# A transformer trunk on one core: the first product behind each LayerNorm, taken part by part in an order set by hand

## The chip, the cores and the metric

One NeuronCore of a Trainium2 chip runs the whole program in one launch. The metric is the device time of one execution in microseconds. The engines are TensorE (PE for matmuls and PEld for its weight loads), VectorE (DVE), ScalarE (ACT), GpSimd (POOL) and SyncE (SP), which issues nearly all DMAs; each engine works through a list of its own, whose order is fixed when the program is compiled.

## What is computed

256 tokens of width 1024 pass through two layers. Layer 0 is a latent attention (MLA), layer 1 a sparse attention whose keys an indexer selects (DSA). Each is followed by PEER, a mixer that finds experts by product keys. Behind each of the four comes a LayerNorm of the residual sum:

```python
for i in range(DEPTH):
    m = _mla_mixer(x, ...) if i % N_MIXERS == 0 else _dsa_mixer(x, ...)
    x = _layernorm(DN_ALPHA * x + m, ln_gain[i, 0], ln_bias[i, 0])
    f = _peer(x, peer_w_q[i], peer_sub_keys[i], peer_w_down[i], peer_w_up[i])
    x = _layernorm(DN_ALPHA * x + f, ln_gain[i, 1], ln_bias[i, 1])
```

`_layernorm` is `(x - mean) * rsqrt(var + eps) * g + b` over the 1024 columns. The first thing that the next mixer does with x is a product: `_peer` has `xt @ w_q`, `_dsa_mixer` has `x @ w_in`.

## The kernel before

**Products in three parts.** Every float32 operand of a large product is held as a rounded high half and a low half, the remainder. A product is then high x high + high x low + low x high, three matmuls into the same PSUM accumulator. `mm` (line 195) issues a matmul.

**The weight stream.** All weights pass through `Stream` as blocks of 128 x 1024 (512 KB), in one fixed order. A block is loaded by SyncE into one of four raw buffers (line 73), ScalarE copies it to the high half (line 85), and raw minus high gives the low half (line 88). There are four buffers each for raw, high and low. A raw buffer is free again when its low split is done; a high or low buffer when TensorE has read it for the last time. The low split runs on VectorE, except that GpSimd takes it for `TO_POOL` = 2 blocks from the moment when the first norm of a pair is written, and for every third block in part of DSA. `ws.get` takes the next block and fills ahead.

**The output products.** `rows` (line 231) multiplies both token tiles (128 tokens each, t = 0 and 1) with one weight block, six matmuls of 512 columns per tile, into four PSUM accumulators y. The last `STAGGER` = 4 blocks are handled in `finish` (line 259): all four for tile 0 first, then all four for tile 1, so that the norm of tile 0 can run beside the products of tile 1.

**The norm.** `layernorm` works on one tile: two halves of the residual sum with their row sums (VectorE, line 248), the negative mean (250), the sum of squares (ScalarE, 251) and the centred rows times the gain (VectorE, 252), the variance (253), its power of -1/2 (GpSimd, 254), and two halves of the result (VectorE, 257).

**The joint.** After a norm, `xpose` turns the tile for the next product: eight TensorE transposes in two groups of four (line 225), each group copied to the high half xh (ScalarE, 211), and its low half xl taken by VectorE (212). The tile is also stored to DRAM (line 229). Then comes the first product of the next stage on its first four weight blocks, `FIRST` = 4: the values of DSA (v, first lines of `dsa`) or the first 512 query columns of PEER (qw, in `peer`). There tile 0 takes its 24 matmuls with all three parts block by block, then tile 1 its 24. There are three such joints: MLA to PEER 0 (joint 1, at about 101 us), PEER 0 to DSA (joint 2, 931 us), DSA to PEER 1 (joint 3, 1071 us). The fourth norm ends in the stores of the output.

In PEER, a query tile is copied to SBUF (line 595), turned by four transposes (qwT, 598), copied again (599), and multiplied with the keys (ps); the keys are loaded at line 584 into memory that the norm's bias held until then. The products on blocks 4 and on follow (pq in PEER; more of v in DSA).

**What sets the order.** The program is written stage by stage; the compiler's list scheduler then orders the instructions of each engine by a simulated time and the dependencies, so an instruction can stand ahead of one that was written earlier. `tc.issue_after(ins)` adds an edge: what is issued in its block stands behind `ins` on the same engine. Before, it is used only to put the last products of tile 1 behind those of tile 0, and around some loads.

Of the kernel before, what the change touches and what calls it, by code (L numbers as in the profile page):

```python
# [22 lines left out]
CHUNK = 64  # L23
DEPTH = 2
HEADS = 8
NKEYS = 128
# [3 lines left out]
ALPHA = (2 * DEPTH) ** 0.25  # L30
LN_EPS = 1e-5
# [9 lines left out]
CELLS = sum(SEG)  # L41
STAGGER = 4
STEPS = (2, 1)
TO_POOL = 2
FIRST = 4
GSCALE = 2.0 ** 14
TINY = 2.0 ** -40
# [4 lines left out]
class Stream:  # L52
# [5 lines left out]
    def __init__(self, nc, raw, hi, lo):  # L58
        self.nc, self.raw, self.hi, self.lo = nc, raw, hi, lo
        self.blocks, self.ready = [], []  # L60
        self.n_loaded = self.n_split = self.n_taken = 0
        self.tiles = []
        self.to_pool = 0
        self.share = 0

    def add(self, src, w=D):
# [10 lines left out]
    def _split(self, upto):  # L77
        nc = self.nc
        while self.n_split <= min(upto, len(self.blocks) - 1):
            w = self.blocks[self.n_split][1]  # L80
            self._load(self.n_split)
            raw = self.tiles[self.n_split][:, :w]
            hi = self.hi.tile([P, D], F32R, tag="hi", name=f"hi{self.n_split}")[:, :w]
            lo = self.lo.tile([P, D], F32R, tag="lo", name=f"lo{self.n_split}")[:, :w]
            nc.scalar.copy(hi, raw)  # L85
            eng = nc.gpsimd if self.to_pool > 0 or (self.share and self.n_split % self.share == 0) else nc.vector
            self.to_pool -= 1
            eng.tensor_tensor(lo, raw, hi.bitcast(F32), op=ALU.subtract)  # L88
            self.ready.append((hi, lo))
            self.n_split += 1  # L90

    def get(self, ahead=None):
        i = self.n_taken
        self.n_taken += 1
        self.fill(i + (self.AHEAD if ahead is None else ahead))
        return self.ready[i]

    def fill(self, upto):
        self._split(upto)
# [31 lines left out]
def tile_trunk(ctx: ExitStack, tc: tile.TileContext, ins, out: bass.AP):  # L131
    nc = tc.nc
# [6 lines left out]
    small = pool("small", 3)  # L139
# [22 lines left out]
    xl = const.tile([P, NC, T], F32R, tag="xl", name="xl")  # L162
# [14 lines left out]
    ws = Stream(nc, raws, his, los)  # L177
# [32 lines left out]
    def split_ps(hi, lo, p):  # L210
        nc.scalar.copy(hi, p)
        return nc.vector.tensor_tensor(lo, p, hi.bitcast(F32), op=ALU.subtract)
# [4 lines left out]
            nc.sync.dma_start(xs[t], src[t])  # L217
        return xs

    def xpose(t, x):  # L220
        for g in range(2):
            p = ps(f"xt{t}{g}")
            for j in range(4):
                c = 4 * g + j
                nc.tensor.transpose(p[:, j * P : (j + 1) * P], x[:, c * P : (c + 1) * P], ident)
            pv = p.rearrange("p (j t) -> p j t", t=P)
            cs, tsl = slice(4 * g, 4 * g + 4), slice(t * P, (t + 1) * P)
            split_ps(xh[:, cs, tsl], xl[:, cs, tsl], pv)
        nc.sync.dma_start(keep[t], x)

    def rows(o4, lhs, blk, start, stop, tiles=(0, 1)):

        h, l = blk
        lh, ll = lhs
        for t in tiles:
            tsl = slice(t * P, (t + 1) * P)
            todo = [(w, rr, i, n) for i, (w, rr) in enumerate(((lh, h), (lh, l), (ll, h))) for n in range(2)]
            if stop:
                todo.sort(key=lambda z: z[3])
            for w, rr, i, n in todo:  # L240
                ins = mm(o4[t][n], w[:, tsl], rr[:, n * 512 : (n + 1) * 512], start and i == 0, stop and i == 2)
        return ins

    def layernorm(x, y2, g, b, r, z, sq):
        st = small.tile([P, 6], F32, tag="st", name="st")
        for n in range(2):
            s = slice(n * 512, (n + 1) * 512)
            nc.vector.scalar_tensor_tensor(r[:, s], x[:, s], ALPHA, y2[n], op0=ALU.mult, op1=ALU.add,
                                           accum_out=st[:, n : n + 1])
        nc.vector.tensor_scalar(st[:, 2:3], st[:, 0:1], st[:, 1:2], -1.0 / D, op0=ALU.add, op1=ALU.mult)  # L250
        nc.scalar.activation(sq, r, AF.Square, bias=st[:, 2:3], accum_out=st[:, 3:4])
        nc.vector.scalar_tensor_tensor(z, r, st[:, 2:3], g, op0=ALU.add, op1=ALU.mult)
        nc.vector.tensor_scalar(st[:, 4:5], st[:, 3:4], 1.0 / D, LN_EPS, op0=ALU.mult, op1=ALU.add)  # L253
        nc.gpsimd.tensor_tensor(st[:, 5:6], st[:, 4:5], mhalf, op=ALU.pow)  # L254
        for n in range(2):
            s = slice(n * 512, (n + 1) * 512)
            nc.vector.scalar_tensor_tensor(r[:, s], z[:, s], st[:, 5:6], b[:, s], op0=ALU.mult, op1=ALU.add)

    def finish(y4, lhs_of, n, g, b, x, spare, after):

        blks = [ws.get(ahead=0) for _ in range(STAGGER)]
        last = None
        for t in range(2):
            with ExitStack() as order:
                if last is not None:
                    order.enter_context(tc.issue_after(last.ins))
                for i, blk in enumerate(blks):
                    k = n - STAGGER + i
                    last = rows(y4, lhs_of(k), blk, k == 0, k == n - 1, (t,))
            layernorm(x[t], y4[t], g, b, spare[t], spare[2 + t], spare[4])  # L270
            if t == 0:
                ws.to_pool = TO_POOL
            after(t, spare[t])

    def load_affine(ar, li, which):
        g, b = ar.take(D), ar.take(D)
# [63 lines left out]
    def out_proj(oh, ol, g, b, x, spare):  # L340
        y4 = [[py(2 * t + n, f"y{t}{n}") for n in range(2)] for t in range(2)]
        for h in range(HEADS - STAGGER):
            rows(y4, (oh[:, h, :], ol[:, h, :]), ws.get(), h == 0, False)
        finish(y4, lambda h: (oh[:, h, :], ol[:, h, :]), HEADS, g, b, x, spare, xpose)

    def load_mask(ar):
        m = ar.take(384)
# [132 lines left out]
    def dsa():  # L480
# [24 lines left out]
        for t in range(2):  # L505
# [8 lines left out]
        p = ps("ki")  # L514
# [50 lines left out]
    def peer(li):  # L565
# [17 lines left out]
        tail = s[0].rearrange("p a b -> p (a b)")  # L583
        nc.sync.dma_start(keys, ins["keys"][li].rearrange("n p k -> p n k"))

        first = [ws.get(ahead=0) for _ in range(FIRST)]
        for t in range(2):
            tsl = slice(t * P, (t + 1) * P)
            p = py(t, f"qw{t}")
            for i, (h, l) in enumerate(first):  # L590
                for j in range(2):
                    c = 2 * i + j
                    half_ = slice(j * 512, (j + 1) * 512)
                    mm3(p, (xh[:, c, tsl], xl[:, c, tsl]), (h[:, half_], l[:, half_]), c == 0, c == NC - 1)
# [4 lines left out]
            nc.scalar.copy(qT[:, 0:4, tsl], p.rearrange("p (n t) -> p n t", t=P))  # L599

        for g4 in range(4):
            for j in range(0, 4 if g4 else 0, 2):
# [158 lines left out]
                g, b = load_affine(lnar, li, 1)  # L761
        spare = [lnar.take(D) for _ in range(5)]

        def store(t, x):
            for n, q in enumerate((nc.sync, nc.scalar)):
                s = slice(n * 512, (n + 1) * 512)
                q.dma_start(out[t * P : (t + 1) * P, s], x[:, s])

        finish(y4, operand, NKEYS, g, b, x, spare, store if last else xpose)

    ws._load(0)
    xt = Arena(arena, 30720).take(NC, T)
# [83 lines left out]
```

## Time and profile before

| | |
|---|---|
| median of 3 runs | 1911.16 us (1910.89 to 1911.22) |
| the profiled execution | 1910.36 us |
| its span | 1908.6 us, 33303 instructions |
| mean granted clock of TensorE | 0.996 |
| TensorE busy with matmuls | 1860.4 us (97%) |
| VectorE | 1358.9 us (71%) |
| ScalarE | 1059.9 us (56%) |
| GpSimd | 582.0 us (30%) |
| DMA | 335.51 MB, mean 176 GB/s |

The span is the stretch from the first to the last instruction of the profiled execution; its time also holds what lies around that, 1.8 us. Matmuls overlap one another, so the busy time of a matmul (some 0.39 us for 512 columns) is longer than the step from one to the next, and the steps have to be read from the starts. A granted clock of 1.00 is 2.4 GHz, 0.50 is 1.2 GHz.

### The profile page before, as it was taken

How to read it: one execution, taken by the hardware profiler on the slowest of the kernel's cores; microseconds unless marked ns; L12 is line 12 of the kernel's file. 1: busy time of each engine (PE TensorE's matmuls, PEld its weight loads, DVE VectorE, ACT ScalarE, POOL GpSimd, SP SyncE). 2: the span in 40 equal slices, each digit the busy share in tenths (PEclk: the TensorE clock that was granted, in tenths of full speed). 3: DMA queues.
4: the chain of work that ended last, by engine and by line, in shares of the span. 5: the costliest groups of instructions: out<-in, count | busy, mean ns of one | idle time of the engine just before them, and what ended most of it. 6: DMA issues, size and time to landing. Idle time of an engine off the chain costs nothing.

```text
span 1908.6 us, 33303 instructions
## 1 busy us (share of the span) xinstructions
PE 1860.4 (97%) x12482; PEld 1674.4 (88%) x12482; DVE 1358.9 (71%) x2765; ACT 1059.9 (56%) x1837; POOL 582.0 (30%) x654
## 2 busy tenths in 40 slices
PE   8989999999999999999998899999999999999998
PEld 8779999999998888888798799999999988888886
DVE  5579998788766555555669689997788765555555
ACT  6544446777655444444466444558777554444443
POOL 2011336999620000000123103359997400000000
PEclk9999999999999999999999999999999999999999
DMA  6354455444446555555554544554444465555553
GB/s 230 120 201 166 154 169 186 156 155 156 166 172 232 190 190 188 188 187 188 183 180 155 172 149 165 179 184 147 155 156 166 167 229 189 188 189 189 190 189 114
DMA packets 93762, 335.51 MB, mean 176 GB/s; under 512 B 10400, under 2 KB 11424, under 8 KB 93600
## 3 DMA queue, kind: packets, MB, share of 16 engines
q1 hardware_dynamic: 93312, 332.87, 50.7%
q8 instruction: 97, 1.59, 0.3%
q14 instruction: 65, 0.53, 0.1%
q10 hardware_dynamic: 288, 0.52, 0.1%
HBM read 329.16 MB, written 4.19 MB: 175 GB/s over the span
## 4 chain that ended last, share of the span: by engine, by line
PE 63%; issue 25%; DVE 7%; POOL 3%; ACT 1%; DMA 1%; SPq 0%; DVEq 0%; POOLq 0%; ACTq 0%
PE d L195 30%; PE y L195 19%; PE pq L195 4%; POOL VU L694 3%; PE G L195 3%; DVE lo L88 2%; PE qw L195 1%; PE v L195 1%; DVE arena L653 1%; PE q L195 1%; PE h L195 1%; PE ps L195 1%; DVE arena L648 1%; PE qi L195 1%; PE qn L195 0%
## 5 line engine op out<-in xcount | busy, mean ns | idle before, releaser
L88 DVE TENSOR_TENSOR lo<-raw,hi 128x1024 fp32r<-128x1024 f32 x593 | 755.4, 1276 | 336.4 <-ACT hi L85 335.4
L85 ACT CAST hi<-raw 128x1024 fp32r<-128x1024 f32 x604 | 631.5, 1048 | 589.4 <-PE y L195 225.2
L195 PE MATMUL d<-xh,lo 128*128 128x256 f32 x2048 | 581.4, 284 | 8.2 <-DVE lo L88 8.2
L195 PE MATMUL d<-xh,hi 128*128 128x256 f32 x2048 | 586.3, 286 | 0.0
L195 PE MATMUL d<-xl,hi 128*128 128x256 f32 x2048 | 579.5, 283 | 0.0
L694 POOL TENSOR_SCALAR VU<-iota,i2t 128x128 f16<-128x128 f16 x512 | 425.8, 849 | 82.0 <-PE G L195 57.4
L195 PEld LDWEIGHTS d<-xh,lo 128*128 128x128 f32 x2048 | 386.7, 189 | 11.0 <-DVE lo L88 11.0
L195 PEld LDWEIGHTS d<-xh,hi 128*128 128x128 f32 x2048 | 387.1, 189 | 0.0
L195 PEld LDWEIGHTS d<-xl,hi 128*128 128x128 f32 x2048 | 386.9, 189 | 0.0
L195 PE MATMUL y<-lo,xh 128*128 128x512 f32 x1088 | 345.2, 395 | 0.0
L195 PE MATMUL y<-hi,xh 128*128 128x512 f32 x1088 | 344.7, 395 | 0.0
L195 PE MATMUL y<-hi,xl 128*128 128x512 f32 x1088 | 344.5, 395 | 0.0
L254 POOL TENSOR_TENSOR st<-st,mhalf 128x1 f32<-128x1 f32 x8 | 4.5, 557 | 863.1 <-DVE st L253 863.1
L195 PEld LDWEIGHTS y<-lo,xh 128*128 128x128 f32 x1088 | 204.8, 188 | 48.0 <-DVE lo L88 0.6
L195 PEld LDWEIGHTS y<-hi,xl 128*128 128x128 f32 x1088 | 205.0, 188 | 47.9
L195 PEld LDWEIGHTS y<-hi,xh 128*128 128x128 f32 x1088 | 204.9, 188 | 47.5
L695 DVE TENSOR_SCALAR VU<-iota,i1t,gt 128x128 f16<-128x128 f16 x512 | 139.3, 346 | 73.2 <-PE G L195 55.4
L696 ACT ACTIVATE U<-VU,gr 128x128 f16<-128x128 f16 x512 | 170.9, 397 | 0.9 <-DVE VU L695 0.5
L750 ACT CAST xh<-arena 128x512 fp32r<-128x512 f32 x128 | 79.3, 620 | 153.1 <-PE y L195 147.8
L751 DVE TENSOR_TENSOR xl<-arena,xh 128x512 fp32r<-128x512 f32 x128 | 88.3, 692 | 80.7 <-ACT xh L750 80.7
L650 POOL TENSOR_TENSOR arena<-arena 128x800 f32<-128x800 f32 x32 | 72.6, 2274 | 96.7 <-DVE arena L648 89.2
L195 PE MATMUL G<-VU 128*128 128x128 f16 x512 | 73.8, 222 | 4.4 <-DVE VU L695 2.2
(220 smaller groups left out, 1869.9 us busy)
## 6 DMA issues: line engine op xcount, KB each, us to landing
raw<-in_down SPq DMA_DIRECT2D x256, 512.0 KB, 3.2
raw<-in_up SPq DMA_DIRECT2D x256, 512.0 KB, 4.2
raw<-in_peer_q SPq DMA_DIRECT2D x32, 512.0 KB, 4.1
raw<-in_dsa_qk SPq DMA_DIRECT2D x16, 512.0 KB, 3.2
raw<-in_mla_w_o SPq DMA_DIRECT2D x8, 512.0 KB, 4.0
raw<-in_dsa_v SPq DMA_DIRECT2D x8, 512.0 KB, 4.1
raw<-in_dsa_w_o SPq DMA_DIRECT2D x8, 512.0 KB, 4.4
raw<-in_mla_qk SPq DMA_DIRECT2D x7, 512.0 KB, 4.8
```

The costliest lines, as they stand in the source:

```text
L85: nc.scalar.copy(hi, raw)
L88: eng.tensor_tensor(lo, raw, hi.bitcast(F32), op=ALU.subtract)
L195: return nc.tensor.matmul(o, l, r, start=start, stop=stop, skip_group_check=True)
L254: nc.gpsimd.tensor_tensor(st[:, 5:6], st[:, 4:5], mhalf, op=ALU.pow)
L648: nc.vector.tensor_tensor(o, iota[:, None, :CELLS].to_broadcast([P, TOPK, CELLS]), posf[t][:, h, :, None].to_broadcast([P, TOPK, CELLS]), ...
L650: nc.gpsimd.tensor_tensor(o, o, cell[t][:, h, None, :].to_broadcast([P, TOPK, CELLS]), op=ALU.mult)
L653: nc.vector.tensor_reduce(exp_[t][:, h - 1, :], held, axis=AX.X, op=ALU.add)
L694: nc.gpsimd.tensor_scalar(V, iota16, i2t[:, t : t + 1], None, op0=ALU.is_equal)
L695: nc.vector.tensor_scalar(U, iota16, i1t[:, t : t + 1], gt[:, t : t + 1], op0=ALU.is_equal, op1=ALU.mult)
L696: nc.scalar.mul(L, U, gr[:, t : t + 1])
L750: nc.scalar.copy(hh, a)
L751: nc.vector.tensor_tensor(al, a, hh.bitcast(F32), op=ALU.subtract)
```

## The change

`TO_POOL` and the counter `to_pool` go: at the joints GpSimd takes no low split any more. `layernorm` becomes the class `Norm`, `xpose` the class `Turned`, with the same instructions, cut into steps that are called one by one. Each step issues through `queue`, which puts every instruction behind the one before it on the same engine (for TensorE, VectorE and ScalarE). `Stream.open` takes a block and issues only its high split, `Stream.close` issues the low split and the load that the raw buffer was kept from. `finish` gets `lead`, which is `lead_queries` or `lead_values` and gives the matmuls of one tile, part and block ("hh", "lh", "hl": first letter the half of x, second the half of the weights), and writes the whole joint out. `dsa` and `peer` take over accumulators that are already begun; in `peer` both query tiles are copied and turned after all 48 matmuls. At the kernel's end (`lead is None`) the two norms follow one another and the stores come behind both.

```diff
-            eng = nc.gpsimd if self.to_pool > 0 or (self.share and self.n_split % self.share == 0) else nc.vector
-            self.to_pool -= 1
+            eng = nc.gpsimd if self.share and self.n_split % self.share == 0 else nc.vector
...
+    def open(self, queue):
+        i = self.n_split
+        self._load(i)
+        raw = self.tiles[i]
+        hi = self.hi.tile([P, D], F32R, tag="hi", name=f"hi{i}")
+        lo = self.lo.tile([P, D], F32R, tag="lo", name=f"lo{i}")
+        queue("act", lambda: self.nc.scalar.copy(hi, raw))
...
+    def close(self, i, queue):
+        hi, lo = self.ready[i]
+        queue("dve", lambda: self.nc.vector.tensor_tensor(lo, self.tiles[i], hi.bitcast(F32), op=ALU.subtract))
+        self._load(i + self.DMA_AHEAD + 1)
...
+    def queue_of():
+        last = {}
+        def queue(engine, emit):
+            with ExitStack() as order:
+                if engine in last:
+                    order.enter_context(tc.issue_after(last[engine]))
+                ins = emit()
+            last[engine] = ins.ins
+            return ins
+        return queue
...
-            layernorm(x[t], y4[t], g, b, spare[t], spare[2 + t], spare[4])
-            if t == 0:
-                ws.to_pool = TO_POOL
-            after(t, spare[t])
+            norms.append(Norm(queue, x[t], y4[t], g, b, spare[t], spare[2 + t], spare[4]))
+        n0, n1 = norms
+        n0.sums()
+        n0.centre()
+        n0.scale()
+        n0.result()
+        if lead is None:
...
+            return
+        nc.sync.dma_start(keep[0], spare[0])
+        queue("pe", lambda: last)
+        x0, x1 = Turned(queue, 0, spare[0]), Turned(queue, 1, spare[1])
+        blk = [ws.open(queue) for _ in range(3)]
+        n1.sums()
+        x0.high(0)
+        x0.high(1)
+        n1.centre()
+        blk.append(ws.open(queue))
+        x0.low(0)
+        n1.scale()
+        x0.low(1)
+        n1.result()
+        nc.sync.dma_start(keep[1], spare[1])
+        unit = lead(queue)
...
+        do(0, "hh", 0, 1, 2)
+        do(0, "lh", 0, 1, 2)
+        do(0, "hh", 3)
+        do(0, "lh", 3)
+        x1.high(0)
+        x1.high(1)
+        do(1, "hh", 0, 1, 2, 3)
+        ws.close(blk[0], queue)
+        ws.close(blk[1], queue)
+        x1.low(0)
+        do(0, "hl", 0, 1)
+        do(1, "lh", 0, 1)
+        do(1, "hl", 0, 1)
+        ws.close(blk[2], queue)
+        x1.low(1)
+        do(0, "hl", 2)
+        do(1, "hl", 2)
+        do(1, "lh", 2)
+        ws.close(blk[3], queue)
+        do(0, "hl", 3)
+        do(1, "hl", 3)
+        do(1, "lh", 3)
...
+    def lead_values(queue):
+        v4 = [[py(2 * t + n, f"v{t}{n}") for n in range(2)] for t in range(2)]
...
+        def unit(t, part, k, blk):
+            l, w = operands(t, part, k, blk)
+            for n in range(2):
+                queue("pe", lambda: mm(v4[t][n], l, w[:, n * 512 : (n + 1) * 512], k == 0 and part == "hh", False))
...
-        v4 = [[py(2 * t + n, f"v{t}{n}") for n in range(2)] for t in range(2)]
-        first = [ws.get(ahead=0) for _ in range(FIRST)]
-        for t in range(2):
-            for c in range(FIRST):
-                rows(v4, (xh[:, c, :], xl[:, c, :]), first[c], c == 0, False, (t,))
+        v4 = begun.pop("v4")
...
-        first = [ws.get(ahead=0) for _ in range(FIRST)]
-        for t in range(2):
-            tsl = slice(t * P, (t + 1) * P)
-            p = py(t, f"qw{t}")
-            for i, (h, l) in enumerate(first):
-                for j in range(2):
-                    c = 2 * i + j
-                    half_ = slice(j * 512, (j + 1) * 512)
-                    mm3(p, (xh[:, c, tsl], xl[:, c, tsl]), (h[:, half_], l[:, half_]), c == 0, c == NC - 1)
-            nc.scalar.copy(qrow[t], p)
+        for t, q in enumerate(begun.pop("q")):
+            nc.scalar.copy(qrow[t], q)
             p = ps(f"qwT{t}")
```

## Rows read from the trace of the kernel before

**Rows 1.** Who was waited for, TensorE alone, whole span. Columns: engine, tile and line that waited <- what it waited for, us in total, times, longest.

```profile
PE qw L195 <- DVE xl L212: 8.1, 2, 4.0
...
PE v L195 <- DVE xl L212: 3.5, 1, 3.5
...
PE xt L225 <- DVE arena L257: 2.7, 3, 1.0
...
PE d L195 <- DVE lo L88: 8.2, 12, 0.8
```

**Rows 2.** Busy time by stretch over joint 2. Columns: the stretch in us, then for PE, PEld, DVE, ACT and POOL the busy us and the number of instructions that start in it, then the granted clock of TensorE (1.00 is 2.4 GHz, 0.50 is 1.2 GHz), the DMA share and GB/s.

```profile
934.00:936.00 2.00, 0.13 (x1) 0.00 (x0) 2.00 (x3) 0.02 (x1) 0.68 (x1) 1.00 0.75 236
...
938.00:940.00 2.00, 2.00 (x6) 1.54 (x6) 1.47 (x3) 0.00 (x0) 0.45 (x1) 0.50 0.79 272
...
940.00:942.00 2.00, 2.00 (x8) 1.65 (x7) 1.41 (x2) 0.00 (x0) 0.10 (x1) 0.76 0.95 381
...
944.00:946.00 2.00, 1.76 (x13) 1.39 (x12) 0.83 (x2) 1.07 (x2) 0.00 (x0) 1.00 0.04 14
```

**Rows 3.** Timeline of joint 2, instructions in order of time, neighbours of one kind merged. Columns: start in us, us, engine, line, operation, out<-in, tile and shape, count, and in brackets the idle time before it and what ended that.

```profile
928.87 3.56 DVE L257 SCALAR_TENSOR_TENSOR arena<-arena,st 128x512 f32<-128x512 f32 x2 [0.69 <-POOL st L254]
...
929.01 5.67 POOL L88 TENSOR_TENSOR lo<-raw,hi 128x1024 fp32r<-128x1024 f32 x2 [0.17 <-ACT hi L85]
...
930.76 0.40 PE L195 MATMUL y<-hi,xl 128*128 128x512 f32 x1
...
932.19 0.58 ACT L211 CAST xh<-xt 128x512 fp32r<-128x512 f32 x1
...
932.96 0.71 PE L195 MATMUL v<-hi,xh 128*128 128x512 f32 x2
...
933.54 3.83 SPq L73 DMA_DIRECT2D raw<-in_dsa_v  x4
...
933.57 2.19 DVE L88 TENSOR_TENSOR lo<-raw,hi 128x1024 fp32r<-128x1024 f32 x1
...
936.94 0.68 DVE L212 TENSOR_TENSOR xl<-xt,xh 128x512 fp32r<-128x512 f32 x1
...
937.67 1.22 PE L195 MATMUL v<-hi,xl 128*128 128x512 f32 x2 [3.54 <-DVE xl L212]
...
943.91 1.03 PE L225 MATMUL xt<-ident,arena 128*128 128x128 f32 x8
...
945.19 0.73 PE L195 MATMUL v<-hi,xh 128*128 128x512 f32 x2 [0.24 <-ACT xh L211]
...
945.75 0.64 PE L195 MATMUL v<-lo,xh 128*128 128x512 f32 x2
...
946.93 1.05 ACT L85 CAST hi<-raw 128x1024 fp32r<-128x1024 f32 x1 [1.31 <-issue]
...
948.01 1.23 DVE L88 TENSOR_TENSOR lo<-raw,hi 128x1024 fp32r<-128x1024 f32 x1 [1.56 <-ACT hi L85]
...
950.88 1.08 PE L195 MATMUL v<-hi,xh 128*128 128x512 f32 x4
```

**Rows 4.** Timeline of the last norm, at the kernel's end, where GpSimd runs no split. Columns as in rows 3.

```profile
1900.44 0.40 PE L195 MATMUL y<-hi,xl 128*128 128x512 f32 x1
...
1901.86 1.28 DVE L252 SCALAR_TENSOR_TENSOR arena<-arena,st 128x1024 f32<-128x1024 f32 x1
...
1901.92 1.15 ACT L251 ACTIVATE arena<-arena,st 128x1024 f32<-128x1024 f32 x1 [4.25 <-DVE st L250]
...
1903.42 0.55 POOL L254 TENSOR_TENSOR st<-st,mhalf 128x1 f32<-128x1 f32 x1 [4.92 <-DVE st L253]
...
1904.01 1.42 DVE L257 SCALAR_TENSOR_TENSOR arena<-arena,st 128x512 f32<-128x512 f32 x2 [0.66 <-POOL st L254]
```

**Rows 5.** Timeline of joint 3. Columns as in rows 3.

```profile
1071.18 0.40 PE L195 MATMUL y<-hi,xl 128*128 128x512 f32 x1
...
1073.27 4.47 SPq L73 DMA_DIRECT2D raw<-in_peer_q  x4
...
1082.48 0.73 SPq L584 DMA_DIRECT2D arena<-in_keys  x1
...
1085.43 0.62 PE L598 MATMUL qwT<-ident,arena 128*128 128x128 f32 x4
...
1091.83 1.05 PE L195 MATMUL ps<-arena 128*128 128x128 f32 x8
...
1093.08 0.36 PE L195 MATMUL pq<-xh,hi 128*128 128x256 f32 x1
```

**Rows 6.** Timeline of joint 1, its last y matmul and the first matmul on block 4. Columns as in rows 3.

```profile
101.42 0.39 PE L195 MATMUL y<-hi,xl 128*128 128x512 f32 x1
...
123.48 0.36 PE L195 MATMUL pq<-xh,hi 128*128 128x256 f32 x1
```

**Rows 7.** DMA issues, whole span. Columns: out<-in, queue, operation, count, KB of each (for the keys, KB of one piece), median us from issue to landing.

```profile
raw<-in_peer_q SPq DMA_DIRECT2D x32, 512.0 KB, 4.1
...
raw<-in_dsa_v SPq DMA_DIRECT2D x8, 512.0 KB, 4.1
...
arena<-in_keys SPq DMA_DIRECT2D x2, 0.5 KB, 6.8
```

More of the change, by code (lines that the diff above doesn't have):

```diff
@@ L43 @@
 STEPS = (2, 1)
-TO_POOL = 2
 FIRST = 4
@@ L62, in __init__ @@
         self.tiles = []
-        self.to_pool = 0
         self.share = 0
@@ L96, in get @@
         return self.ready[i]
+    def open(self, queue):
+        i = self.n_split
+        assert i == self.n_taken
+        self._load(i)
[3 more added lines that the diff above has]
+        queue("act", lambda: self.nc.scalar.copy(hi, raw))
+        self.ready.append((hi, lo))
+        self.n_split += 1
+        self.n_taken += 1
+        return i
+    def close(self, i, queue):
+        hi, lo = self.ready[i]
+        queue("dve", lambda: self.nc.vector.tensor_tensor(lo, self.tiles[i], hi.bitcast(F32), op=ALU.subtract))
+        self._load(i + self.DMA_AHEAD + 1)
     def fill(self, upto):
@@ L218, in load_x @@
         return xs
[L220 to L229, printed above, removed]
     def rows(o4, lhs, blk, start, stop, tiles=(0, 1)):
@@ L242, in rows @@
         return ins
[L244 to L257, printed above, removed]
@@ L259, in finish, with __init__, sums, centre @@
-    def finish(y4, lhs_of, n, g, b, x, spare, after):
+    def queue_of():
[8 more added lines that the diff above has]
+        return queue
+    class Norm:
+        def __init__(self, queue, x, y2, g, b, r, z, sq):
+            self.queue, self.x, self.y2, self.g, self.b, self.r, self.z, self.sq = queue, x, y2, g, b, r, z, sq
+            self.st = small.tile([P, 6], F32, tag="st", name="st")
+        def sums(self):
+            st = self.st
+            for n in range(2):
+                s = slice(n * 512, (n + 1) * 512)
+                self.queue("dve", lambda: nc.vector.scalar_tensor_tensor(
+                    self.r[:, s], self.x[:, s], ALPHA, self.y2[n], op0=ALU.mult, op1=ALU.add,
+                    accum_out=st[:, n : n + 1]))
+            self.queue("dve", lambda: nc.vector.tensor_scalar(st[:, 2:3], st[:, 0:1], st[:, 1:2], -1.0 / D,
+                                                              op0=ALU.add, op1=ALU.mult))
+        def centre(self):
+            st = self.st
+            self.queue("act", lambda: nc.scalar.activation(self.sq, self.r, AF.Square, bias=st[:, 2:3],
+                                                           accum_out=st[:, 3:4]))
+            self.queue("dve", lambda: nc.vector.scalar_tensor_tensor(self.z, self.r, st[:, 2:3], self.g,
+                                                                     op0=ALU.add, op1=ALU.mult))
+        def scale(self):
+            st = self.st
+            self.queue("dve", lambda: nc.vector.tensor_scalar(st[:, 4:5], st[:, 3:4], 1.0 / D, LN_EPS,
+                                                              op0=ALU.mult, op1=ALU.add))
+            nc.gpsimd.tensor_tensor(st[:, 5:6], st[:, 4:5], mhalf, op=ALU.pow)
+        def result(self):
+            for n in range(2):
+                s = slice(n * 512, (n + 1) * 512)
+                self.queue("dve", lambda: nc.vector.scalar_tensor_tensor(
+                    self.r[:, s], self.z[:, s], self.st[:, 5:6], self.b[:, s], op0=ALU.mult, op1=ALU.add))
@@ new lines, in tile_trunk, with __init__, where, high @@
+    class Turned:
+        def __init__(self, queue, t, x):
+            self.queue, self.t, self.x, self.p = queue, t, x, {}
+        def where(self, g):
+            return slice(4 * g, 4 * g + 4), slice(self.t * P, (self.t + 1) * P)
+        def high(self, g):
+            p = ps(f"xt{self.t}{g}")
+            for j in range(4):
+                c = 4 * g + j
+                self.queue("pe", lambda: nc.tensor.transpose(p[:, j * P : (j + 1) * P],
+                                                             self.x[:, c * P : (c + 1) * P], ident))
+            self.p[g] = p.rearrange("p (j t) -> p j t", t=P)
+            cs, ts = self.where(g)
+            self.queue("act", lambda: nc.scalar.copy(xh[:, cs, ts], self.p[g]))
+        def low(self, g):
+            cs, ts = self.where(g)
+            self.queue("dve", lambda: nc.vector.tensor_tensor(xl[:, cs, ts], self.p[g], xh[:, cs, ts].bitcast(F32),
+                                                              op=ALU.subtract))
@@ L261, in finish @@
+    def finish(y4, lhs_of, n, g, b, x, spare, lead=None):
         blks = [ws.get(ahead=0) for _ in range(STAGGER)]
+        queue = queue_of()
         last = None
+        norms = []
         for t in range(2):
@@ L269, in finish @@
                     last = rows(y4, lhs_of(k), blk, k == 0, k == n - 1, (t,))
-            layernorm(x[t], y4[t], g, b, spare[t], spare[2 + t], spare[4])
-            if t == 0:
-                ws.to_pool = TO_POOL
-            after(t, spare[t])
+            norms.append(Norm(queue, x[t], y4[t], g, b, spare[t], spare[2 + t], spare[4]))
[9 more added lines that the diff above has]
+            n1.result()
+            for t in range(2):
+                for h, q in enumerate((nc.sync, nc.scalar)):
+                    s = slice(h * 512, (h + 1) * 512)
+                    q.dma_start(out[t * P : (t + 1) * P, s], spare[t][:, s])
+            return
@@ new lines, in finish, with do @@
+        nc.sync.dma_start(keep[0], spare[0])
+        queue("pe", lambda: last)
+        x0, x1 = Turned(queue, 0, spare[0]), Turned(queue, 1, spare[1])
+        blk = [ws.open(queue) for _ in range(3)]
+        n1.sums()
+        x0.high(0)
+        x0.high(1)
+        n1.centre()
+        blk.append(ws.open(queue))
+        x0.low(0)
+        n1.scale()
+        x0.low(1)
+        n1.result()
+        nc.sync.dma_start(keep[1], spare[1])
+        unit = lead(queue)
+        def do(t, part, *ks):
+            for k in ks:
+                unit(t, part, k, ws.ready[blk[k]])
@@ new lines, in finish, with operands @@
+        do(0, "hl", 3)
+        do(1, "hl", 3)
+        do(1, "lh", 3)
+    def operands(t, part, c, blk):
+        tsl = slice(t * P, (t + 1) * P)
+        return (xh if part[0] == "h" else xl)[:, c, tsl], blk[0 if part[1] == "h" else 1]
+    def lead_values(queue):
+        v4 = [[py(2 * t + n, f"v{t}{n}") for n in range(2)] for t in range(2)]
+        begun["v4"] = v4
+        def unit(t, part, k, blk):
+            l, w = operands(t, part, k, blk)
+            for n in range(2):
+                queue("pe", lambda: mm(v4[t][n], l, w[:, n * 512 : (n + 1) * 512], k == 0 and part == "hh", False))
+        return unit
@@ L275, in load_affine, with lead_queries, unit @@
+    def lead_queries(queue):
+        q = [py(t, f"qw{t}") for t in range(2)]
+        begun["q"] = q
+        def unit(t, part, k, blk):
+            for j in range(2):
+                l, w = operands(t, part, 2 * k + j, blk)
+                queue("pe", lambda: mm(q[t], l, w[:, j * 512 : (j + 1) * 512], k + j == 0 and part == "hh",
+                                       k == FIRST - 1 and j == 1 and part == ("hl" if t == 0 else "lh")))
+        return unit
+    begun = {}
     def load_affine(ar, li, which):
@@ L343, in out_proj @@
             rows(y4, (oh[:, h, :], ol[:, h, :]), ws.get(), h == 0, False)
-        finish(y4, lambda h: (oh[:, h, :], ol[:, h, :]), HEADS, g, b, x, spare, xpose)
+        finish(y4, lambda h: (oh[:, h, :], ol[:, h, :]), HEADS, g, b, x, spare, lead_queries)
     def load_mask(ar):
@@ L762, in peer @@
         spare = [lnar.take(D) for _ in range(5)]
[L764 to L769, printed above, removed]
+        finish(y4, operand, NKEYS, g, b, x, spare, None if last else lead_values)
     ws._load(0)
```

2 lines of the change are left out of this document (1 added, 1 removed).

## The prediction

> **What bounds the kernel now.** I read the page first: TensorE is busy 97% of the span, the other engines far less, so time can only come out of the places where TensorE stands still. The list of who waited for whom, for TensorE alone [rows 1], says where: the long single waits are 4.0, 4.0 and 3.5 us, all for the low half of the turned activations (xl, line 212), each with about 0.9 us more for the end of the norm (line 257). That is one place, met three times: the joint behind each norm that a further product follows. I call the joint at 931 us (into the sparse-attention values) joint 2; those at 101 and 1071 us (into the PEER queries) are joints 1 and 3.
>
> The table of stretches over joint 2 [rows 2] shows what is lost: in 934 to 936 us one matmul starts, and afterwards the granted clock is 0.50, with 6 starts in 2 us (938 to 940) and 8 in the next 2, against 10 in a full 2 us. So the wait is paid twice, as idle time and as about 2 + 4 = 6 missing matmuls.
>
> The timeline says why [rows 3]. The last matmul of y starts at 930.76, and 24 + 24 matmuls of the new product and 16 transposes follow. Pitch: 22 matmuls from 945.75 to 950.88, 0.233 us each; transposes: 8 in 1.03, 0.13 each. Full-speed work: 48 x 0.233 + 16 x 0.13 = 13.3 us. The next work starts at 950.88, which is 20.1 us after the last y; 0.24 of it is that matmul's own turn. So 20.1 - 13.5 = **6.6 us** is lost in this joint. VectorE is the late one: the two result halves took 3.56 us while GpSimd ran its two low splits (929.01, 5.67 us), against 1.42 us for the same pair with GpSimd idle, in the last norm [rows 4]; a VectorE low split took 2.19 us beside GpSimd and 1.23 us alone [rows 3]. Behind both, xl comes only at 936.94.
>
> **The change, with L the start of the last y matmul** (930.76 in joint 2). Durations are those of rows 3 and 4. Three edits act as one chain, so I lay it out engine by engine.
>
> *GpSimd's two low splits go to VectorE.* That adds 2 x 1.23 = 2.5 us of VectorE work per joint, and frees it of contention. The result of tile 0 then starts at 928.87 as before and ends at 930.29, which is L - 0.47, 2.1 us earlier than now.
>
> *TensorE* therefore goes straight into the 8 transposes of tile 0 (L + 0.24 to 1.3). ScalarE turns the first four into xh by L + 1.43 (0.58 each, as at 932.19), and the first matmul started 0.19 us after that in the trace (932.77 to 932.96): L + 1.65. The six high-by-high matmuls of blocks 0 to 2 end at L + 3.05.
>
> *VectorE*: the sums of tile 1 cannot start before y ends; in the last norm the centring starts 1.42 us after the last y matmul starts (1900.44 to 1901.86) [rows 4]. Centring L + 1.42 to 2.70; x0.low(0) to 3.38. TensorE's low-by-high matmuls of blocks 0 to 2 can thus run L + 3.4 to 4.8. ScalarE: two copies to 2.05, square to 3.2 plus 0.1 for its sum, fourth high split to 4.35. VectorE: scale 3.4, GpSimd's power 3.65 to 4.2 (0.55), x0.low(1) inside that to 4.3, result of tile 1 4.3 to 5.72. TensorE: block 3, both parts, 4.8 to 5.75; then tile 1's transposes, 5.75 to 6.8; xh of tile 1 at 6.95; eight high-by-high matmuls 7.1 to 8.97. VectorE: low splits of blocks 0 and 1 to 6.95 and 8.2, x1.low(0) to 8.85, block 2 to 10.1, x1.low(1) to 10.75, block 3 to 12.0. TensorE wants these at 8.97, 9.4, 9.9, 11.8 and 13.2, so they are hidden with 0.1 to 1.7 us to spare, and the last 24 matmuls run through: 8.97 to **L + 14.55**.
>
> Before, that point lay at L + 20.12 [rows 3]. **Joint 2: -5.57 us**, and 1 us of loss stays (the copy of xh twice, and the centring).
>
> *Joints 1 and 3* have the same 48 matmuls, but a tail. Now the transposes of the first query tile (0.53 us, 1085.43) lie in a gap between the tiles; pq starts at 1093.08 = L + 21.9 with only tile 1's score products (1.05 us, as those at 1091.83) still to come [rows 5]. Afterwards both tiles end together: transposes of q0 at 14.55 to 15.1, those of q1 after its 0.6 us copy, about 15.45 to 16.0, score products after the copies 16.1 to 18.2, then pq. 21.9 + 1.05 - 18.2 = **-4.75 us** in joint 3, and for joint 1 (101.42 to 123.48 = 22.06) **-4.9 us** [rows 6]. If pq's matmuls are put into the two small gaps instead, 0.45 us more; I take the order shown now, which puts the transposes first.
>
> *Weight loads move later*, the cost that the chain hides. A raw buffer comes free when its low split is done: now the four next loads start at 933.54 (L + 2.8) [rows 3], afterwards at about L + 7.0, 8.2, 10.1 and 12.0. They are hidden by the 24 matmuls behind them. A load landed 4.1 us after its issue in the median [rows 7]; block 4 then arrives at 11.1, its high split waits for hi buffer 0 (read until L + 10.8) and ends at 12.2, its low split at 13.4; it is wanted at 14.55. No cost up to 5.2 us to landing; up to the largest median of these rows, 6.8, it is 1.6 us a joint. I take 0, since the weights' own rows say 4.1.
>
> *Keys*: 6.8 us to landing [rows 7], waiting for the norm's bias to be read, now at 1082.48 = L + 11.3, afterwards from L + 5.8; they land at 12.6 and are wanted at 16.1. Cost 0, if SyncE issues them when they are ready, ahead of the loads (as it does now with the loads that were ready first); bounds 0 and 2.8 (below).
>
> *The last norm* keeps its chain. Tile 0's store may now be issued behind tile 1's square on ScalarE; it still goes out before tile 1's: 0. What else in the kernel waits [rows 1] is untouched: 0, with the 8.2 us of low-split waits in the d stage as the nearest size for a shift of the compiled order there, either way.
>
> **Sum**: 5.57 + 4.75 + 4.9 = 15.2 us. The profiled execution took 1910.36 us (span 1908.6), 0.8 below the median of the three runs. 1910.36 - 15.2 = 1895.2 there, 1896.0 on the median. A change within 0.2% (3.8 us) is what a measurement can hardly tell from none.
>
> **A rule against it.** In the trace the clock fell after the 3.5 us wait with nothing but VectorE's work, and not around the 1.3 us of eight transposes and a short wait at 943.91 to 945.19: 944 to 946 was granted 1.00 [rows 2, 3]. Afterwards no stretch without matmuls is longer than about 1.4 us (L + 0.24 to 1.65, 5.75 to 7.1), so I let the clock stay. The Trainium skill (TensorE: Matmul & The Clock Gate, Part 4: PE-mode transpose) says that transposes don't count as TensorE activity in the way matmuls do; by that the two stretches would count as idle from end to end and could bring the clock down. The row at 944 us speaks against it, for a stretch of that length.
>
> **The rivals.**
> - *The clock falls anyway.* Six matmuls lost in each joint, as now [rows 2]: 6 x 0.233 x 3 = 4.2 us back, 1900. Against: the row at 944 us. Chance 0.06.
> - *The queries' tail becomes the wait.* SyncE issues the keys behind the four weight loads (L + 12): they land at 18.9 instead of 12.6 and the score products wait 2.8 us, twice: 5.6 back, 1901.6. For: in joint 3 the loads did stand ahead of the keys (1082.48). Against: they were ready first then; now the keys are. Chance 0.15.
> - *The next weights come late.* Place: block 4 behind each joint. Decision point: 5.2 us from issue to landing costs nothing; up to 7.5 gives back some 2 us a joint, 1898 to 1903 (chance 0.12). Beyond 10.8 us all 5.57 are gone, and at 12 us the kernel is slower, 1911 + 3 x 1.2 = 1915. For: four loads, the stored tile and the keys crowd into 7 us. Against: no median among the landing times shown is above 6.8 [rows 7]. Chance of slower 0.04.
> - *The order by hand does little.* If the compiler's list already had TensorE as early as it can be, or if the hand's chains only reproduce it, what is left is small: 1907 to 1911. Against: 6.6 us of idle time and lost clock in a joint whose inputs are late only by VectorE's order and GpSimd's contention. Chance 0.03.
>
> **How the numbers follow.** The forecast, all three joints close to 5 us, 0.60: 1892.5 to 1899. Its lower end is TensorE never waiting: 20.1 - 13.5 = 6.6 in joint 2, about 5.8 in the others, 18.2 in all, 1893, and half a microsecond for the runs. The range reaches up over the clock, the keys and the mild weights, 1892.5 to 1903. Faster by over 0.2% is the forecast, the clock, the tail and the mild weights, 0.93; within 0.2% is the order that does little, 0.03; slower 0.04.
>
> **What would show it.** Right: TensorE's waits for xl behind qw and v gone; granted clock 1.00 through all three joints; the result pair at 1.4 us for tile 0 too and no low split on GpSimd there; 14 to 15 us from the last y matmul to the matmuls on block 4. Wrong: a new TensorE wait for a low split of block 4, or for keys, in its place; a clock of 0.50 behind the transposes; VectorE splits still at 2.2 us; or a gain in the joints that returns as low-split waits in the d stage.

## The result and the profile after

The changed kernel takes **1901.38 us** in the median of five runs (1900.2 to 1904.22), against 1911.22 for the kernel before in the same set: a ratio of 0.9947, interval 0.9932 to 0.9961. That is 9.8 us less, where 15.2 were forecast; 1901.4 lies inside the range given (1892.5 to 1903), but outside the band of the forecast itself (1892.5 to 1899, all three joints close to 5 us). The profiled execution took 1900.2 us (span 1898.4).

Who was waited for, TensorE alone, whole span, columns as in rows 1. The waits for xl behind qw and v [rows 1] are gone; what is left of the joint itself is 0.2 us at a time. The low-split waits of the d stage (PEER's product with its down weights) are where they were. But there is a new line, qwT, which waits 1.6 to 1.8 us for ScalarE's copy of the first query tile and 0.8 us for that of the second, in two joints:

```profile
PE qwT L741 <- ACT arena L738: 4.9, 4, 1.8
...
PE qw L211 <- ACT xh L316: 1.0, 4, 0.2
...
PE d L211 <- DVE lo L85: 7.7, 12, 0.8
```

**Joint 2 went as laid out.** Its timeline, columns as in rows 3 (L = 927.57, the last y matmul):

```profile
925.67 1.42 DVE L296 SCALAR_TENSOR_TENSOR arena<-arena,st 128x512 f32<-128x512 f32 x2 [0.69 <-POOL st L291]
...
927.57 0.40 PE L211 MATMUL y<-hi,xl 128*128 128x512 f32 x1
...
929.08 1.67 PE L211 MATMUL v<-hi,xh 128*128 128x512 f32 x6 [0.24 <-ACT xh L316]
...
930.18 0.68 DVE L320 TENSOR_TENSOR xl<-xt,xh 128x512 fp32r<-128x512 f32 x1
...
930.92 1.66 PE L211 MATMUL v<-hi,xl 128*128 128x512 f32 x6 [0.18 <-DVE st L289]
...
931.59 1.41 DVE L296 SCALAR_TENSOR_TENSOR arena<-arena,st 128x512 f32<-128x512 f32 x2
...
934.62 2.13 PE L211 MATMUL v<-hi,xh 128*128 128x512 f32 x8 [0.24 <-ACT xh L316]
...
942.19 1.10 PE L211 MATMUL v<-hi,xh 128*128 128x512 f32 x4
```

The result pair of tile 0 takes 1.42 us, not 3.56 [rows 3]. The first six matmuls start at L + 1.51, xl comes at L + 2.61 (TensorE's 0.18 us of waiting for it bears the name st, the small step that VectorE does between the two halves of xl), tile 1's matmuls start at L + 7.05, and block 4's first matmul at 942.19 = L + 14.62 (forecast 14.55, before 20.12 [rows 3]). The granted clock is 1.00 in every stretch of 2 us there.

**Joints 1 and 3 did not.** The timeline of joint 3 (L = 1062.55); SPq is SyncE's queue:

```profile
1062.55 0.39 PE L211 MATMUL y<-hi,xl 128*128 128x512 f32 x1
...
1068.55 0.72 SPq L735 DMA_DIRECT2D arena<-in_keys  x1
...
1069.39 20.78 SPq L71 DMA_DIRECT2D raw<-in_peer_q  x9
...
1076.68 0.63 PE L211 MATMUL qw<-hi,xl 128*128 128x512 f32 x2
...
1077.48 1.04 ACT L83 CAST hi<-raw 128x1024 fp32r<-128x1024 f32 x1 [7.44 <-DMA raw<-in_peer_q]
...
1078.43 0.58 ACT L738 COPY arena<-qw 128x512 f32<-128x512 f32 x1
...
1078.91 1.05 ACT L83 CAST hi<-raw 128x1024 fp32r<-128x1024 f32 x1
...
1079.07 0.66 PE L741 MATMUL qwT<-ident,arena 128*128 128x128 f32 x4 [1.75 <-ACT arena L738]
...
1079.86 0.59 ACT L738 COPY arena<-qw 128x512 f32<-128x512 f32 x1
...
1080.50 1.11 PE L741 MATMUL qwT<-ident,arena 128*128 128x128 f32 x4 [0.78 <-ACT arena L738]
...
1081.27 0.56 PE L211 MATMUL pq<-xh,hi 128*128 128x256 f32 x1
...
1084.54 1.05 PE L211 MATMUL ps<-arena 128*128 128x128 f32 x8
```

The 48 matmuls end on time: the last pair starts at 1076.68, so TensorE is free at 1077.15 = L + 14.6. ScalarE then should copy the query tile, but the compiler has put the high split of block 4 ahead of the copy (1077.48), and ScalarE stood idle for 7.44 us before it, at the end for its load. The copy starts at 1078.43, the transposes at 1079.07, and a second split (1078.91) parts the two copies. pq starts at 1081.27 = L + 18.7, with all of the score products (2 x 1.05 us) still to come. And the clock falls (columns as in rows 2; the number in brackets, here as there, counts the instructions that run in the stretch, also those begun before it):

```profile
1076.00:1078.00 2.00, 1.31 (x6) 0.75 (x4) 0.00 (x0) 0.52 (x1) 0.00 (x0) 1.00 1.02 410
...
1078.00:1080.00 2.00, 0.66 (x4) 0.42 (x4) 1.23 (x2) 2.00 (x4) 0.00 (x0) 1.00 0.68 270
...
1080.00:1082.00 2.00, 1.50 (x7) 1.50 (x8) 1.31 (x2) 2.00 (x4) 0.00 (x0) 0.55 0.59 193
...
1082.00:1084.00 2.00, 2.00 (x13) 2.00 (x12) 1.79 (x2) 1.31 (x2) 0.00 (x0) 0.59 0.86 219
```

Between 1078 and 1080 no product matmul starts, only four transposes; then the granted clock is 0.55 and 0.59 for two stretches of 2 us, and the pq matmuls step by 0.21 us instead of 0.12: eleven of them, 1.0 us. The second four transposes, too, take 0.77 us up to the next matmul instead of 0.41 in joint 1. Joint 1 has the same tail (L = 101.72, pq at L + 18.26), in this execution at full clock:

```profile
101.72 0.39 PE L211 MATMUL y<-hi,xl 128*128 128x512 f32 x1
...
118.14 0.66 PE L741 MATMUL qwT<-ident,arena 128*128 128x128 f32 x4 [1.64 <-ACT arena L738]
...
119.98 0.36 PE L211 MATMUL pq<-xh,hi 128*128 128x256 f32 x1
```

**The account.** Joint 2: 20.12 - 14.62 = 5.5 us. Joint 1: 22.06 + 1.05 [rows 5, 6] - (18.26 + 2.1) = 2.75. Joint 3: 21.9 + 1.05 - (18.72 + 2.1) - 1.0 for the clock = 1.1. Together 9.4 of the 10.2 us between the two profiled executions; no other stretch, before, between or behind the joints, differs by more than 0.75 us.

### The profile page after: what moved, and what is told of

It reads as the page before. It is cut to its first block, busy times and chain, and to the rows that moved or that the text cites. A ratio compares the mean times of both kernels' runs of the same rounds, so it can differ in the third digit from the quotient of the medians.

```text
span 1898.4 us, 33300 instructions
## 1 busy us (share of the span) xinstructions
PE 1858.9 (98%) x12482; PEld 1673.4 (88%) x12482; DVE 1356.6 (71%) x2771; ACT 1058.3 (56%) x1837; POOL 565.4 (30%) x648
## 4 chain that ended last, share of the span: by engine, by line
PE 85%; DVE 9%; issue 2%; POOL 1%; ACT 1%; DMA 1%; SPq 0%; DVEq 0%; POOLq 0%; ACTq 0%
PE y L211 40%; PE d L211 31%; PE pq L211 4%; PE G L211 3%; DVE lo L85 3%; PE v L211 1%; PE q L211 1%; POOL VU L837 1%; PE s L211 1%; DVE arena L791 1%; DVE arena L796 1%; PE ps L211 1%; PE qw L211 1%; PE qi L211 1%; PE h L211 1%
## 5 line engine op out<-in xcount | busy, mean ns | idle before, releaser
L85 DVE TENSOR_TENSOR lo<-raw,hi 128x1024 fp32r<-128x1024 f32 x587 | 745.4, 1272 | 340.4 <-ACT hi L83 338.6
L83 ACT CAST hi<-raw 128x1024 fp32r<-128x1024 f32 x592 | 619.3, 1048 | 600.1 <-PE y L211 224.3
```

## The experiments

Two questions: which part of the change makes the 5.5 us of a joint, and where the other 5 us of the forecast went. The forecast's rivals had placed a loss in the tail by late keys, or behind it by late weights; the trace shows neither as such. Theory A: the order on ScalarE. Theory B: the load of block 4 is late because keys and stored tile are issued ahead of it. Theory C: the copies and transposes of two tiles that end together are the limit.

The first four kernels ran on one chip (before: 1911.89 us, 15 runs), the other four on another (1911.07, 19 runs).

**The copies first (e1_copies).**

```diff
-            nc.scalar.copy(qrow[t], q)
+            copied = nc.scalar.copy(qrow[t], q)
...
+        with tc.issue_after(copied.ins):
+            ws.fill(ws.n_taken + 3)
         for g4 in range(4):
```

> The kernel after, with the splits of the blocks behind the joint put behind the copies of both query tiles on ScalarE. In the kernel after, the next product starts 18.3 us (joint 1) and 18.7 us (joint 3) after the last y matmul, with 2.1 us of score products still to come, and TensorE waits 1.6 to 1.8 us for the first copy. Theory A, the order on ScalarE alone: the high split of block 4 stands ahead of the copies and waits for its load, so with the copies first the product starts at 16.3 in both joints and the clock stays: 5.4 us less, 1896. Theory B, the load of block 4 is late because the keys and the stored tile go ahead of it: the copies no longer wait, but the product then waits for block 4's low split until about 18: 1 us less, 1900.

Measured: 1897.41 us (1897.25 to 1899.38), ratio 0.9925 (0.9912 to 0.9939): 4 us less than the change (4.2 by the two ratios), between the two forecasts. Joint 3, L = 1062.16:

```profile
1076.79 0.60 PE L741 MATMUL qwT<-ident,arena 128*128 128x128 f32 x4
...
1078.57 0.39 PE L211 MATMUL pq<-xh,hi 128*128 128x256 f32 x1 [0.29 <-ACT hi L83]
...
1079.83 0.39 PE L211 MATMUL pq<-xh,lo 128*128 128x256 f32 x1 [0.76 <-DVE lo L85]
```

The transposes start at L + 14.63, so the wait for the copy was the order on ScalarE, as A says. pq starts at L + 16.41 with its first two matmuls, and then waits 0.76 us for block 4's low split, as B says, until 17.67; joint 1 is the same within 0.02 us. The clock stays at 1.00.

**The keys early (e2_keys).** The keys get memory that no norm uses, so their load can be issued long before: in the profiled execution it is issued at 82.7 and 838.6 us, ahead of joint 1's norm by 19 us and of joint 3's by over 200.

```diff
-        qT, keys = ar.take(16, T), ar.take(16, NKEYS)
+        qT = ar.take(16, T)
         s = [ar.take(16, NKEYS) for _ in range(2)]
+        keys = ar.take(16, NKEYS)
```

> The kernel after, with the keys in memory that is free long before the joint, so that their load is no longer issued between the joint's stores and block 4. Theory B: block 4 lands 4 to 5 us after its issue instead of 8, about 11.5 us after the last y matmul; what is left is the order on ScalarE, where now the split of block 6 stands ahead of the first copy: next product at 17.3, clock stays, 3.4 us less, 1898. Theory A: the order is what counts, and with three splits ahead of the copy the tail stays at 18 or grows: no gain, 1901.

Measured: 1896.36 us (1895.65 to 1899.48), ratio 0.992 (0.9907 to 0.9934): 5 us less than the change, more than B forecast. Time from issue to landing of the loads for blocks 4 to 7 in joint 3, first in the changed kernel:

```profile
DMA to landing us min/median/max: 7.4/7.7/8.0
```

and with the keys early:

```profile
DMA to landing us min/median/max: 3.4/4.4/4.7
```

In both kernels the store of tile 1 (0.5 MB) is issued just ahead of these loads; what is gone from there is the 1 MB of keys, so the keys cost the next loads 3.3 us. Joint 3, L = 1061.36:

```profile
1075.66 1.05 ACT L83 CAST hi<-raw 128x1024 fp32r<-128x1024 f32 x1 [1.00 <-DMA raw<-in_peer_q]
...
1076.61 1.07 ACT L739 COPY arena<-qw 128x512 f32<-128x512 f32 x2
...
1078.15 0.36 PE L211 MATMUL pq<-xh,hi 128*128 128x256 f32 x1
```

pq now starts at L + 16.8 in both joints, though three splits stand ahead of the first copy (in joint 3 the last of them waits 1.00 us for its load). By the trace the early load alone does a little more than the order alone, where pq started at 16.41 and then waited until 17.67; the two medians lie 1 us apart and their intervals overlap, so the times do not show it.

**Both (e3_both).** Keys early as in e2; blocks 4 and 5 split ahead of the copies, 6 and 7 behind.

```diff
+        ws.fill(ws.n_taken + 1)
+        with tc.issue_after(copied.ins):
+            ws.fill(ws.n_taken + 3)
```

> Both edits: keys early, blocks 4 and 5 split before the copies and blocks 6 and 7 behind them. Theories A and B together: next product 16.3 us after the last y matmul in joints 1 and 3, granted clock 1.00 there, 5.4 us less than the kernel after, 1896. Rival C, the chain of copies and transposes of two tiles that end together is the limit whatever the loads do: no earlier than 18, 1900 to 1901.

Measured: **1894.64 us** (1894.35 to 1898.25), ratio 0.9913 (0.9899 to 0.9926), the fastest of all. Joint 3, L = 1060.53:

```profile
1075.18 0.60 PE L742 MATMUL qwT<-ident,arena 128*128 128x128 f32 x4
...
1076.02 0.66 PE L742 MATMUL qwT<-ident,arena 128*128 128x128 f32 x4 [0.24 <-ACT arena L739]
...
1076.43 0.36 PE L211 MATMUL pq<-xh,hi 128*128 128x256 f32 x1
```

Transposes at 14.65, pq at 15.90: from the last of the 48 matmuls on TensorE waits 0.24 us once. Clock 1.00. C falls: the two tiles that end together cost 0.24 us of waiting. The median is 6.7 us under that of the change (by the two ratios, 0.9947 - 0.9913, 6.5), where 5.4 was expected. The trace accounts for 6.2 of it: 2.35 in joint 1, 2.82 in joint 3 and 1.0 for joint 3's clock.

**GpSimd's splits alone (e4_pool).** The kernel before with one number changed.

```diff
-TO_POOL = 2
+TO_POOL = 0
```

> The kernel before with one part of the change alone: GpSimd takes no low split at the joints, everything else as before. Theory, the order by parts is what pays: the result pair of tile 0 falls from 3.56 to 1.4 us, but VectorE has two splits more ahead of xl, so xl comes at most 1 us earlier: 1908 to 1911. Rival, the contention with GpSimd is the cause: 2.1 us at the result pair and 0.95 us at a split in each joint, and the clock does not fall: 9 to 13 us less, 1898 to 1902.

Measured: 1912.11 us (1908.64 to 1913.92), ratio 0.9999 (0.999 to 1.0008): nothing, where 1 to 4 us less was expected. Joint 2, L = 932.66:

```profile
930.77 1.42 DVE L257 SCALAR_TENSOR_TENSOR arena<-arena,st 128x512 f32<-128x512 f32 x2 [0.69 <-POOL st L254]
...
932.10 2.36 DVE L88 TENSOR_TENSOR lo<-raw,hi 128x1024 fp32r<-128x1024 f32 x2
...
935.59 2.36 DVE L88 TENSOR_TENSOR lo<-raw,hi 128x1024 fp32r<-128x1024 f32 x2
...
937.86 1.28 DVE L212 TENSOR_TENSOR xl<-xt,xh 128x512 fp32r<-128x512 f32 x2
...
938.60 0.73 PE L195 MATMUL v<-hi,xl 128*128 128x512 f32 x2 [2.68 <-DVE xl L212]
...
951.86 1.10 PE L195 MATMUL v<-hi,xh 128*128 128x512 f32 x4
```

The result pair is fast, but VectorE spends the time on four low splits (two pairs of 2.36 us) that stand ahead of xl. xl comes at L + 5.2 instead of 6.18 [rows 3], the wait is 2.68 us instead of 3.54, and block 4 comes at L + 19.2, 0.9 us earlier. In the query joints TensorE's longest wait for xl falls as well, from 4.0 [rows 1] to 3.1 us, but pq stands at L + 22.1 and 21.8 as before (22.06 and 21.9).

**GpSimd's splits back, all else as changed (e5_pool_back).** `close` of the first two blocks uses GpSimd:

```diff
-        ws.close(blk[0], queue)
-        ws.close(blk[1], queue)
+        ws.close(blk[0], queue, pool=True)
+        ws.close(blk[1], queue, pool=True)
```

> The kernel after, with one part undone: GpSimd takes the low splits of the first two blocks at each joint again, the order by parts and by hand stays. Theory, the contention costs on the path that the parts leave: the result pair of tile 0 takes 3.5 us again, the 48 matmuls end about 16.5 us after the last y matmul instead of 14.6; their raw buffers come free earlier, which shortens the tail of the queries by some 2 us: 1903 to 1907. Rival, the contention is worth nothing once the parts are in order: 14.6 as now, and with the shorter tail 1897 to 1899.

Measured: 1904.34 us (1903.58 to 1906.24), ratio 0.9963 (0.995 to 0.9976); the change on that chip 1901.36. Joint 2, L = 930.03:

```profile
928.14 3.54 DVE L299 SCALAR_TENSOR_TENSOR arena<-arena,st 128x512 f32<-128x512 f32 x2 [0.69 <-POOL st L294]
...
933.18 1.84 DVE L287 SCALAR_TENSOR_TENSOR arena<-arena,st 128x1024 f32<-128x1024 f32 x1
...
935.68 2.24 PE L214 MATMUL v<-hi,xl 128*128 128x512 f32 x6 [1.82 <-DVE st L292]
...
948.49 1.09 PE L214 MATMUL v<-hi,xh 128*128 128x512 f32 x4
```

The result pair is back at 3.54 us, the centring of tile 1 takes 1.84 instead of 1.28, TensorE waits 1.82 for xl (again under the name st), the clock falls to 0.63 and 0.52 (936 to 940), and block 4 comes at L + 18.46, 3.8 us late. I had put that at 1.9: the clock and the centring were not in it. In the whole it is 3.0 us more than the change by the medians and 1.9 by the two ratios, whose intervals overlap; what shows the loss is joint 2. In the query joints, where the loads of blocks 4 and 5 start earlier again, pq comes at L + 19.8 and 19.5, only 0.8 to 1.6 us later than in the changed kernel.

**By hand, but tile by tile (e6_by_tile).**

```diff
         x0.low(0)
+        ws.close(blk[0], queue)
+        ws.close(blk[1], queue)
+        x0.low(1)
+        ws.close(blk[2], queue)
+        ws.close(blk[3], queue)
         n1.scale()
-        x0.low(1)
...
+        def do(t, *parts):
+            for k in range(4):
+                for part in parts:
+                    unit(t, part, k, ws.ready[blk[k]])
+        do(0, "hh", "lh", "hl")
...
+        do(1, "hh", "hl", "lh")
```

> The kernel after with the order by hand but not by parts: tile 0 takes all three parts of block 0, then of block 1 and so on, then tile 1; VectorE does the low halves of x and all four low splits of the weights before tile 1's scale. Theory, the parts pay (high by high can run while the low halves are made): TensorE waits for the first low split until 4.6 us and for tile 1's transposes until 11.5, the 48 matmuls end at 18.4 instead of 14.6; about 1.7 us per joint under the kernel before: 1904 to 1908. Rival, it is only the order of VectorE and ScalarE that pays: 15 us and 1900 to 1902.

Measured: 1907.97 us (1904.98 to 1909.17), ratio 0.9979 (0.997 to 0.9989). Joint 2, L = 929.66:

```profile
933.02 0.73 PE L211 MATMUL v<-hi,xl 128*128 128x512 f32 x2 [1.12 <-DVE xl L320]
...
934.15 0.73 PE L211 MATMUL v<-lo,xh 128*128 128x512 f32 x2 [0.40 <-DVE lo L111]
...
939.73 1.29 PE L312 MATMUL xt<-ident,arena 128*128 128x128 f32 x8 [0.58 <-DVE arena L296]
...
946.73 1.10 PE L211 MATMUL v<-hi,xh 128*128 128x512 f32 x4
```

Short waits for xl (1.12), the first low split (0.40) and tile 1's result (0.58), and block 4 at L + 17.07: better than the 18.4 I had worked out, 2.45 us later than by parts. Two things change together here, since tile by tile TensorE wants the low splits early: VectorE does all four ahead of tile 1's result, which starts at L + 9.17 instead of 4.02. In both query joints the score products, now early, waited for the keys' load (1.19 and 2.79 us), which stands behind the four weight loads: the forecast's second rival, in another kernel. So part of the whole time is the keys', not the parts', and that it lies in the range expected shows little; the price of the parts is read from joint 2.

**The order on TensorE alone (e7_pe_only).**

```diff
-                if engine in last:
+                if engine in last and engine == "pe":
```

> The kernel after with the order by hand kept on TensorE only; VectorE and ScalarE stand in the order that the compiler gives them, which puts all four low splits of the weights and tile 1's sums ahead of the low halves of x. Theory, parts and order pay only together: low half of x at 6.5 us, result of tile 1 at 11.3, the 48 matmuls end at about 20 as in the kernel before: 1908 to 1912. Rival, the parts on TensorE carry the gain: 14.6 to 16 us and 1901 to 1904.

Measured: 1906.71 us (1905.38 to 1907.09), ratio 0.9975 (0.9965 to 0.9985). Joint 2, L = 930.20:

```profile
933.12 2.35 DVE L111 TENSOR_TENSOR lo<-raw,hi 128x1024 fp32r<-128x1024 f32 x2
...
935.40 1.28 DVE L320 TENSOR_TENSOR xl<-xt,xh 128x512 fp32r<-128x512 f32 x2
...
936.13 2.05 PE L211 MATMUL v<-hi,xl 128*128 128x512 f32 x6 [2.20 <-DVE xl L320]
...
949.08 1.08 PE L211 MATMUL v<-hi,xh 128*128 128x512 f32 x4
```

The compiler's order puts the low splits of the weights ahead of xl; TensorE waits 2.20 us and loses clock behind it (0.80 and 0.50 from 936 to 940); block 4 at L + 18.88 (I had said 20), pq in the query joints at L + 19.99 and 19.78. The time lies between the two forecasts and in neither. Of joint 2's 5.5 us the parts on TensorE alone bring 1.2 and the order by hand tile by tile 3.05: neither carries the gain alone.

**The change again (e0_after).**

> The kernel after again, unchanged, on the chip of this set, as the level that the other three are read against: 1901.4, 48 matmuls done 14.6 us after the last y matmul, next product at 18.3 and 18.7 in the query joints.

Measured: 1901.36 us (1900.31 to 1908.07), ratio 0.9953 (0.9941 to 0.9965); pq at L + 18.75 and 18.65. Here the clock fell in joint 1 too:

```profile
120.00:122.00 2.00, 2.00 (x11) 2.00 (x10) 1.31 (x2) 2.00 (x4) 0.00 (x0) 0.50 0.76 268
```

## Why the prediction was right, and where it was off

*The bound.* Right. The three waits for xl were the loss. In joint 2, where nothing follows but the same product, all of the forecast gain came: 5.5 of 5.57 us. One reading was off: the numbers in brackets of [rows 2] are not starts. By the starts, no matmul begins in 934 to 936, and 5 and 6 in the two stretches from 938 on, against 2 / 0.233 = 8.6; that makes about 6 missing again, so the price of the clock stands.

*The chain, step by step.* Right within 0.15 us at TensorE's steps (first matmul L + 1.51 for 1.65, tile 1's at 7.05 for 7.1, the end at 14.62 for 14.55). VectorE came ahead of the plan, by 0.3 us at tile 1's result (4.02 for 4.3) and by 0.8 us at the end of the last low split (11.17 for 12.0), which only made its spare larger. GpSimd's splits were costed as a part of one chain, and e4 and e5 show why that was needed: removing them alone gives nothing (0.9999), putting them back costs 2 to 3 us of the whole and 3.8 in joint 2. Block 4 in joint 2 stands at L + 20.1 before, 19.2 without GpSimd's splits, 18.9 with the order on TensorE only, 18.5 with GpSimd's splits back, 17.1 tile by tile and 14.6 with everything: each part missing costs 2.5 to 4.3 us.

*The clock.* Right for the joint: the trace granted 1.00 through both stretches of transposes there. It was wrong for the tail, which I had laid out with 1.5 us between product matmuls (L + 14.55 to 16.1). There eight transposes and waits of 1.64 to 1.76 and 0.78 us left 3.7 to 4.1 us without a product matmul (from L + 14.6 on), and in three of the four such tails in two profiled executions the clock fell to 0.50. The Trainium skill (TensorE: Matmul & The Clock Gate, Part 4: PE-mode transpose) says that transposes don't count as TensorE activity in the way matmuls do. The tails and the joint's 1.3 us stretches both leave room for that, but in a tail the transposes cannot be told from the waits beside them, so no run here shows it.

*The tail of joints 1 and 3*: this step failed. I forecast 4.75 and 4.9 us, and got 1.1 and 2.75. I worked out the copies, transposes and score products as if ScalarE had nothing else in its list, after having put block 4's high split in the same stretch myself. "Weight loads move later" took 4.1 us to landing from the whole-span median [rows 7]; with keys and stored tile ahead it was 7.4 to 8.0, which by my own decision point (5.2) was a cost. And here a split that waited for its load held up all that ScalarE had behind it. The mixture was in the rivals as two separate ones (keys behind the loads; late weights), and it was the reverse of the first: the keys were on time because the loads stood behind them. e1, e2 and e3 show that the tail, not the joint, held the missing gain: with both repaired the kernel is 6.5 to 6.7 us faster than the change, and 5.8 us of the tail's forecast were missing. In e3 the two query joints give 5.1 and 4.95 us by the account used above, against 4.9 and 4.75 forecast: the terms of the tail were right once no split held up the copies.

*Luck.* The second rival's 1901.6 is within 0.3 us of the measured time, but its mechanism, keys behind the loads, did not occur. The time fell into the range because that reached over the rivals, not because the forecast's sum held.

What stays open: the 0.8 us between the account and the two executions, and why joint 1's clock fell in one execution of the same kernel and not in the other: the first wait was 1.64 us where it held, and 1.67 to 1.76 in the three tails where it fell, too little between them to tell.

## What to carry to other kernels

When a chain of small steps between two products is late, lay out all engines from one common event and ask of every instruction not only when its inputs are there but what stands ahead of it in its engine's list; a step that waits for a transfer must not stand ahead of a step that the critical engine waits for. Here, splitting a product so that its first part needs only what is ready first paid in full only when the engines that make the rest were ordered to match, and each of these alone may show little: of joint 2's 5.5 us, GpSimd's part alone brought 0.9 and nothing of the whole, the parts on TensorE alone 1.2. Take the landing time of a load from a stretch in which the same other transfers are queued, not from a median over the program.

## What the runs showed of the hardware

- In a tail that held eight transposes and two waits, 3.7 to 4.1 us without a product matmul, the clock fell to 0.50 in three cases of four (the changed kernel, two executions); the pq matmuls behind each fall took 1.0 to 1.2 us longer.
- While GpSimd subtracted 128 x 1024 blocks, VectorE instructions with two SBUF inputs took 3.54 us for a pair that takes 1.42, and 1.84 us for one of 1.28 (e5 against the change).
- 1 MB of keys issued ahead of them in the joint lengthened four 512 KB loads from 4.4 to 7.7 us (medians, e2 and the change; a 0.5 MB store stood ahead in both).
